# SwiGLU gate and up as seven products of block sums in a transformer block

## Chip, cores and metric

The kernel runs on one core of a Trainium2 chip. The metric is the device time of one execution in microseconds (us). The median of three runs is given; the profile is of one further execution. All arithmetic is in 32-bit floats; matmuls take their operands in the fp32r format.

## The reference

One encoder layer over 512 tokens (plus 16 learned ones that attention alone sees) of width 1024: a norm, a joint projection, two attention branches, gates and an output projection, then the feed-forward part, in which the change lies:

```
hn = rmsnorm(h, norm_ffn_g)                                   # 512 tokens x 1024
h  = h + (silu(hn @ w_ffn_gate) * (hn @ w_ffn_up)) @ w_ffn_down   # D_FF = 2816
y  = rmsnorm(h, norm_final_g)
```

## The kernel before

**Precision by three products.** Every large matmul is made of three: each 32-bit operand is split into a high half (a ScalarE cast to fp32r) and a low half (VectorE: the value less its high half), and `mm3` (L142) adds high x high, high x low and low x high into one PSUM bank. `split` (L73) is the helper that makes the two halves; its cast is L74 and its subtraction L75.

**Weights.** All weights are one list, `stream`, of chunks of 512 KB in the order in which they are used. `stage` (L119) issues a chunk's load on SyncE's queue into one of three buffers `wst`; `weights(key)` (L132) loads STAGE = 5 chunks ahead and splits READY = 2 chunks ahead into one of four pairs of buffers `wh`, `wl`. A chunk of gate (`fg`, f) or up (`fu`, f) holds 1024 rows (8 blocks k of 128) by 128 columns, a chunk of the down projection holds 2 blocks k by 512 columns.

**Stages.** After attention comes the output projection (`accumulate` with "out"): two halves of the output columns, the first in banks of the pool `z`, the second in banks of the pool `mm`. The second half ends token block by token block; each end adds to the residual `hres` (L805), takes the sum of squares (L808) and the reciprocal root (`rstd`), scales to `hn` (L825). `turned(tp)` (L827) transposes half the tokens of `hn` on TensorE, four 128x128 blocks to a bank, and ScalarE (L838) and VectorE (L839) take the bank out as `hT_h` and `hT_l`, 8 blocks k by 512 tokens. Gate and up of feature block 0 (`early`) are computed in two halves of 256 tokens, to fill TensorE's time around the second `turned`.

The feed-forward loop then runs over the other 21 blocks f of 128 features. For each, gate and up are 8 blocks k x 3 matmuls of 512 tokens, 48 in all; ScalarE applies SiLU (L872), VectorE multiplies (L876) and the result is split into `aT_h`, `aT_l`. Last comes the down projection (`accumulate` with "down"): 22 blocks k, 4 token blocks, two halves of the output columns; then the final norm and the stores.

**Order.** Outside a hand-ordered opening, a planner sets the order on each engine: of the instructions that it takes to be ready it issues the one that stands first in the program. `high_priority(offset=EVAC)` moves an instruction ahead. Buffers, and whole pools that take over the space of pools closed before, wait for the release of what they replace. PSUM has four banks under `mm` and two tiles of two banks under `z`.

Of the kernel before, what the change touches and what calls it, by code (L numbers as in the profile page):

```python
# [9 lines left out]
F32 = mybir.dt.float32  # L10
F32R = mybir.dt.float32r
# [5 lines left out]
P = 128  # L17
# [22 lines left out]
def block_kernel(ctx: ExitStack, tc: tile.TileContext, x, meta, norm_mix_g, w_in, w_gate, b_gate,  # L40
# [18 lines left out]
    def tr_tile():  # L59
        return ps_mm.tile([P, 512], F32, tag="mm", name="tr")  # L60
# [52 lines left out]
    for half in range(2):  # L113
        for k0 in range(0, NFF, 2):
            rows(("down", half, k0), w_fd, half * 512, k0)

    staged, loaded = [], {}

    def stage(upto):  # L119
        for n in range(len(staged), min(len(stream), upto)):  # L120
            _, view, c0, cw, k0, k1 = stream[n]
            st = wpool.tile([P, k1 - k0, cw], F32, tag="wst", bufs=3, name="wst")
            staged.append(st)
            for a, b in ((0, 4), (4, 8)) if n < 2 else ((0, k1 - k0),):
                nc.sync.dma_start(st[:, a:b], view[:, k0 + a:k0 + b, c0:c0 + cw])

    def parts(n):
        k, _, _, cw, k0, k1 = stream[n]
        loaded[k] = tuple(wpool.tile([P, k1 - k0, cw], F32R, tag=t, name=t) for t in ("wh", "wl"))
        return loaded[k]  # L130

    def weights(key):  # L132
        at = next(i for i, c in enumerate(stream) if c[0] == key)
        if at < START:
            return loaded[key]
        stage(at + STAGE)
        for n in range(len(loaded), min(len(stream), at + READY)):
            wh, wl = parts(n)
            split(wh, wl, staged[n], nc.gpsimd if n < 3 else None)
        return loaded[key]  # L140

    def mm3(ps, pairs, start=True, stop=True):  # L142
        n = len(pairs)
        for i, (ah, al, bh, bl) in enumerate(pairs):
            nc.tensor.matmul(ps, lhsT=ah, rhs=bh, start=(start and i == 0), stop=False)  # L145
            nc.tensor.matmul(ps, lhsT=ah, rhs=bl, start=False, stop=False)  # L146
            nc.tensor.matmul(ps, lhsT=al, rhs=bh, start=False, stop=(stop and i == n - 1))  # L147

    def proj(ps, w, act, tok, ks=(0, KT)):
        (wh, wl), (ah, al) = w, act  # L150
# [624 lines left out]

    def accumulate(pool, name, act, nk, half, tail, done, banks, pieces=None):

        ah, al = act
# [5 lines left out]
        extra = z_tile()[:, 0] if pieces else None  # L784

        def step(k, t, c0, c1):
            wh, wl = weights((name, half, k // 2 * 2))
            q = slice(t * P, (t + 1) * P)
            mm3((acc[t] if c0 == 0 else extra)[:, c0:c1],
                [(ah[:, k, q], al[:, k, q], wh[:, k % 2, c0:c1], wl[:, k % 2, c0:c1])], k == 0, k == nk - 1)  # L790


        def cuts(t):
# [26 lines left out]
    with tc.tile_pool(name="outp", bufs=1) as op_:  # L820
        hn = op_.tile([P, NQ, D], F32, name="hn")

        def normed(t):
            r = rstd(ssq[t][:, 1:2], more=ssq[t][:, 0:1])()
            nc.vector.tensor_scalar(hn[:, t], hres[:, t], r, None, op0=ALU.mult)  # L825

        def turned(tp):  # L827
            cs = slice(tp * 256, (tp + 1) * 256)
            for k in range(0, KT, 2):
                pt = tr_tile()  # L830
                for i in range(2):
                    for t in range(2):
                        nc.tensor.transpose(pt[:, (2 * i + t) * P:(2 * i + t + 1) * P],  # L833
                                            hn[:, 2 * tp + t, (k + i) * P:(k + i + 1) * P], ident)
                for i in range(2):
                    g = g_ffn[:, k + i:k + i + 1]
                    p = pt[:, i * 256:(i + 1) * 256]
                    nc.scalar.activation(hT_h[:, k + i, cs], p, AF.Copy, scale=g)  # L838
                    nc.vector.scalar_tensor_tensor(hT_l[:, k + i, cs], p, g, hT_h[:, k + i, cs].bitcast(F32),  # L839
                                                   op0=ALU.mult, op1=ALU.subtract)  # L840

        def done(t):
            normed(t)
            if t == 2:
                turned(0)

        accumulate(op_, "out", (mg_h, mg_l), KT, 0, 0, lambda t: None, "z")
        accumulate(op_, "out", (mg_h, mg_l), KT, 1, 6, done, "mm")

        early = [mm_tile(), mm_tile()]  # L850
        for ps, key in zip(early, (("fg", 0), ("fu", 0))):
            proj(ps[:, 0:256], weights(key), hT, slice(0, 256))
        turned(1)
        for ps, key in zip(early, (("fg", 0), ("fu", 0))):
            proj(ps[:, 256:512], weights(key), hT, slice(256, 512))
        use_table("silu_and_others")
    mid.close()


    with tc.tile_pool(name="ffn", bufs=1) as fp:  # L860
        aT_h = fp.tile([P, NFF, SEQ], F32R, name="aT_h")
        aT_l = fp.tile([P, NFF, SEQ], F32R, name="aT_l")
        gF = fp.tile([P, D], F32, name="gF")
        nc.gpsimd.dma_start(gF, norm_final_g.rearrange("(o d) -> o d", o=1).broadcast_to([P, D]))
        for f in range(NFF):
            if f == 0:
                pg, pu = early
            else:
                pg = mm_tile()
                proj(pg, weights(("fg", f)), hT, ALL)  # L870
            sg = fp.tile([P, SEQ], F32, tag="sg", bufs=2, name="sg")
            nc.scalar.activation(sg, pg, AF.Silu)  # L872
            if f:
                pu = mm_tile()
                proj(pu, weights(("fu", f)), hT, ALL)
            nc.vector.tensor_tensor(sg, pu, sg, op=ALU.mult)  # L876
            split(aT_h[:, f], aT_l[:, f], sg)
# [12 lines left out]

        def gained(t, cs):
            if len(outs) == t:
                outs.append(fp.tile([P, D], F32, tag="outs", name="outs", bufs=2))
# [4 lines left out]
        accumulate(fp, "down", (aT_h, aT_l), NFF, 0, 0, lambda t: None, "z")  # L898
        accumulate(fp, "down", (aT_h, aT_l), NFF, 1, 6, finish, "mm", gained)


# [27 lines left out]
```

## Time and profile before

| | us |
|---|---|
| median of 3 runs | 1004.76 (1004.44 to 1005.29) |
| profiled execution, its own time | 1004.22 |
| span of the profile | 1002.5 |
| TensorE busy | 986.8 |
| VectorE busy | 526.5 |
| ScalarE busy | 451.0 |
| first transposes of `hn` to last of gate and up | 625 to 874 |
| down projection to the end | 874 to 1002.5 |

Engines: PE is TensorE, PEld its weight loads, DVE VectorE, ACT ScalarE, POOL GpSimd, SP SyncE; SPq and POOLq are DMA queues. A row of the view by line gives line, engine, operation, written tile <- read tiles, shapes and count, then busy time and the mean of one in ns, then idle time of the engine before them and what ended it. A row of the timeline gives start and duration in us, then the instruction. TensorE's matmuls overlap, so the distance between two starts tells more than one matmul's duration.

### The profile page before, as it was taken

The numbers are of one execution on the slowest core, as the hardware profiler recorded it, in microseconds if no ns is written. First come the engines' busy times: TensorE is split into PE (matmuls) and PEld (weight loads), VectorE is DVE, ScalarE is ACT, GpSimd is POOL, SyncE is SP. The second block draws the span as 40 slices with busy tenths as digits, with TensorE's granted clock in tenths as the row PEclk, the third lists the DMA queues.
The fourth block names the chain that finished last, engine by engine and source line by source line (L and its number), as shares of the span: only waits on it lengthen the run. The fifth ranks groups of instructions, "written<-read, shape, count | busy, mean of one in ns | idle before, by whom it ended". The sixth has DMA issues, their size and how long they took to land.

```text
span 1002.5 us, 14077 instructions
## 1 busy us (share of the span) xinstructions
PE 986.8 (98%) x5529; PEld 855.2 (85%) x5529; DVE 526.5 (53%) x974; ACT 451.0 (45%) x848; POOL 109.9 (11%) x152
## 2 busy tenths in 40 slices
PE   7999999999999999999999999999999999999997
PEld 5999899998889999889878888888888888888886
DVE  7665446667777777777763334633333333312323
ACT  5655564555455666555653333623232232311313
POOL 4000000000122121122013220000000000000103
PEclk9999999999999999999999999999999999999998
DMA  6322222222333332333223352433333333232212
GB/s 198 106 64 63 85 85 63 85 64 64 86 105 86 106 85 65 105 85 86 84 84 85 104 177 76 122 91 103 99 91 105 87 103 103 87 105 88 102 42 85
DMA packets 129733, 93.01 MB, mean 93 GB/s; under 512 B 3681, under 2 KB 114434, under 8 KB 129666
## 3 DMA queue, kind: packets, MB, share of 16 engines
q1 hardware_dynamic: 127506, 85.09, 28.2%
q0 software_dynamic: 2000, 6.95, 2.6%
q8 instruction: 43, 0.70, 0.3%
q14 instruction: 24, 0.20, 0.1%
q10 hardware_dynamic: 160, 0.07, 0.0%
HBM read 85.67 MB, written 2.10 MB: 88 GB/s over the span
## 4 chain that ended last, share of the span: by engine, by line
PE 93%; DVE 3%; ACT 2%; issue 0%; DMA 0%; POOL 0%; SPq 0%; DVEq 0%; ACTq 0%; POOLq 0%
PE mm L145 25%; PE mm L146 24%; PE mm L147 24%; PE z L145 4%; PE z L146 4%; PE z L147 4%; PE tr L301 2%; PE z L432 1%; PE z L433 1%; PE tr L276 1%; PE z L325 0%; PE tr L313 0%; DMA xs<-in_x_dram 0%; PE tr L833 0%; DVE xs L608 0%
## 5 line engine op out<-in xcount | busy, mean ns | idle before, releaser
L75 DVE TENSOR_TENSOR wl<-wst,wh 128x1024 fp32r<-128x1024 f32 x150 | 185.8, 1239 | 256.8 <-ACT wh L74 254.3
L74 ACT CAST wh<-wst 128x1024 fp32r<-128x1024 f32 x150 | 157.9, 1052 | 358.7 <-PE mm L146 267.5
L145 PE MATMUL mm<-xT_h,wh 128*128 128x264 f32 (+2 forms) x776 | 249.1, 321 | 1.0 <-DVE dk L413 0.8
L146 PE MATMUL mm<-xT_l,wh 128*128 128x264 f32 (+2 forms) x776 | 246.9, 318 | 0.4 <-DVE xT_l L619 0.3
L147 PE MATMUL mm<-xT_h,wl 128*128 128x264 f32 (+2 forms) x776 | 246.1, 317 | 0.0
L145 PEld LDWEIGHTS mm<-xT_h,wh 128*128 128x128 f32 x776 | 146.1, 188 | 11.7 <-ACT xT_h L618 1.0
L146 PEld LDWEIGHTS mm<-xT_l,wh 128*128 128x128 f32 x776 | 146.0, 188 | 10.1 <-DVE xT_l L619 0.7
L147 PEld LDWEIGHTS mm<-xT_h,wl 128*128 128x128 f32 x776 | 146.0, 188 | 10.0
L146 PE MATMUL mm<-hT_l,wh 128*128 128x512 f32 (+1 forms) x368 | 139.9, 380 | 0.0
L145 PE MATMUL mm<-hT_h,wh 128*128 128x512 f32 (+1 forms) x368 | 139.7, 380 | 0.1
L147 PE MATMUL mm<-hT_h,wl 128*128 128x512 f32 (+1 forms) x368 | 139.7, 380 | 0.0
L145 PEld LDWEIGHTS mm<-hT_h,wh 128*128 128x128 f32 x368 | 69.0, 188 | 13.6 <-ACT hT_h L838 0.4
L146 PEld LDWEIGHTS mm<-hT_l,wh 128*128 128x128 f32 x368 | 69.2, 188 | 13.2 <-DVE hT_l L839 0.2
L147 PEld LDWEIGHTS mm<-hT_h,wl 128*128 128x128 f32 x368 | 69.2, 188 | 13.1
L145 PE MATMUL mm<-o_h,wh 128*128 128x512 f32 x128 | 53.2, 415 | 0.0
L876 DVE TENSOR_TENSOR sg<-mm,sg 128x512 f32<-128x512 f32 x22 | 15.2, 691 | 70.8 <-PE mm L147 70.8
L146 PE MATMUL mm<-o_l,wh 128*128 128x512 f32 x128 | 50.1, 391 | 0.8 <-DVE o_l L504 0.8
L147 PE MATMUL mm<-o_h,wl 128*128 128x512 f32 x128 | 50.1, 391 | 0.0
L282 POOL COPY v_s<-vT 128x16 f32<-128x16 f32 x64 | 21.8, 369 | 210.0 <-ACT vT L287 210.0
L460 ACT ACTIVATE pr<-pr,nm 128x144 f32<-128x144 f32 (+3 forms) x64 | 36.3, 568 | 14.2 <-DVE nm L458 14.1
L145 PE MATMUL z<-wh,aT_h 128*128 128x512 f32 (+1 forms) x110 | 40.5, 368 | 0.0
L146 PE MATMUL z<-wl,aT_h 128*128 128x512 f32 (+1 forms) x110 | 40.5, 368 | 0.0
(227 smaller groups left out, 1538.3 us busy)
## 6 DMA issues: line engine op xcount, KB each, us to landing
wst<-in_w_in_dram SPq DMA_DIRECT2D x46, 512.0 KB, 3.9
wst<-in_w_ffn_gate_dram SPq DMA_DIRECT2D x22, 512.0 KB, 3.8
wst<-in_w_ffn_up_dram SPq DMA_DIRECT2D x22, 512.0 KB, 3.8
wst<-in_w_ffn_down_dram SPq DMA_DIRECT2D x22, 512.0 KB, 3.6
wst<-in_w_gate_dram SPq DMA_DIRECT2D x16, 512.0 KB, 3.9
dk<-dk POOLq DMA_DIRECT2D x16, 264.0 KB, 4.9
wst<-in_w_br_sb_dram SPq DMA_DIRECT2D x8, 512.0 KB, 3.5
wst<-in_w_br_df_dram SPq DMA_DIRECT2D x8, 512.0 KB, 3.6
```

Of the source, the lines that this page charges most:

```text
L74: (hi_copy or nc.scalar.copy)(hi, src)
L75: (lo_eng or nc.vector).tensor_tensor(lo, src, hi.bitcast(F32), op=ALU.subtract)
L145: nc.tensor.matmul(ps, lhsT=ah, rhs=bh, start=(start and i == 0), stop=False)
L146: nc.tensor.matmul(ps, lhsT=ah, rhs=bl, start=False, stop=False)
L147: nc.tensor.matmul(ps, lhsT=al, rhs=bh, start=False, stop=(stop and i == n - 1))
L276: nc.tensor.transpose(pt[:, j * P:(j + 1) * P], vT[:, j * P:(j + 1) * P], ident)
L282: nc.gpsimd.tensor_copy(v_s[:, 32 * t:32 * t + NM], vT[:, (t + 1) * P:(t + 1) * P + NM])
L301: nc.tensor.transpose(pt[:, (t - j) * P:(t - j + 1) * P], blocks(t, j * P, (j + 1) * P), ident)
L432: nc.tensor.matmul(o, lhsT=q[c][:, qs], rhs=k[c][:, 0, k0:k1], start=True, stop=False)
L433: nc.tensor.matmul(o, lhsT=q[c][:, qs], rhs=k[c][:, 1, k0:k1], start=False, stop=True)
L460: nc.scalar.activation(pr[:, c], pr[:, c], AF.Exp, bias=nm[:, c:c + 1], accum_out=ls[:, t, c:c + 1])
L876: nc.vector.tensor_tensor(sg, pu, sg, op=ALU.mult)
```

## The change

For each feature block f from 1 on, gate and up together are a product of two 2x2 block matrices: rows gate and up by columns K1 and K2 (the first and last four blocks k) on the weights' side, and K1 and K2 by T1 and T2 (the first and last 256 tokens) on the activations' side. Instead of eight block products, seven products of sums are made (the Strassen-Winograd scheme), each of 4 blocks k x 3 matmuls of 256 tokens: 84 matmuls a block f.

- Activations: `turned` also copies each transposed piece, unsplit, to `bf` (16 more ScalarE instructions); `block_sums` makes three sums and one intermediate on VectorE and splits the four operands that are not slices of `hT` or are negated (t2, t1, t3, t4).
- Weights: up is loaded a second time in part: K1 to the tile `s21`, onto which an accumulating DMA from GpSimd's queue adds K2; a second accumulating DMA adds gate's K1 onto up's K1 in its staging tile `wsu`. VectorE makes the other two sums (in `c2` and `c4`). Jobs `c1` to `c4` split gate; s2 and s1; s3 and up's K2; s4.
- Products: `first` (a11·b11, a12·b21), `second` (s2·t2, s1·t1, s3·t3), `third` (a22·t4, s4·b22); the next block's `first` stands between `second` and `third`. One bank, e1, goes through four products in turn and is copied out by ScalarE in between.
- The feed-forward result `aT` is kept unsplit; the down projection splits each block k when it needs it (`act`), in each of its two halves, into 8 buffers `da` of a pool `dw`.

The core of the diff:

```diff
@@ stage
+            if key[0] == "fu" and key[1]:
+                if "w" not in fpools:
+                    return
+                st = fpools["w"].tile([P, KT, P], F32, tag="wsu", bufs=2, name="wsu")
+                s21 = fpools["w"].tile([P, KT, P], F32, tag="s21", bufs=3, name="s21")
+                fpools["s", key[1]] = s21
+            else:
+                st = wpool.tile([P, k1 - k0, cw], F32, tag="wst", bufs=3, name="wst")
...
+            if key[0] == "fu" and key[1]:
+                cs = slice(c0, c0 + cw)
+                nc.sync.dma_start(s21[:, 4:8], view[:, 0:4, cs])
+                nc.gpsimd.dma_start(s21[:, 4:8], view[:, 4:8, cs], accum_op=ALU.add)
+                nc.gpsimd.dma_start(st[:, 0:4], w_fg[:, 0:4, cs], accum_op=ALU.add)
@@ turned, block_sums
+                nc.scalar.activation(bf[k // 4][tp_][:, (k + i) % 4], p, AF.Copy, scale=g)
+    def block_sums():
+        (b11, b12), (b21, b22) = bf
+        sub, add = ALU.subtract, ALU.add
+        nc.vector.tensor_tensor(b11, b11, b12, op=sub)
+        nc.vector.tensor_tensor(b12, b22, b12, op=sub)
+        nc.vector.tensor_tensor(b22, b11, b22, op=add)
+        nc.vector.tensor_tensor(b21, b22, b21, op=sub)
+        th, tl = tsum["t2"]
+        nc.scalar.activation(th, b22, AF.Copy, scale=-1.0)
+        nc.vector.scalar_tensor_tensor(tl, b22, -1.0, th.bitcast(F32), op0=ALU.mult, op1=sub)
+        for n, v in (("t1", b11), ("t3", b12), ("t4", b21)):
+            split(*tsum[n], v)
@@ feed-forward
+        def c1(f):
+            wh, wl = chunk(1)
+            split(wh, wl, staged[at_of["fg", f]])
...
+        def c2(f):
+            g = staged[at_of["fg", f]]
+            s = fpools["s", f]
+            nc.vector.tensor_tensor(s[:, K1], s[:, K2], g[:, K1], op=ALU.add)
+            wh, wl = chunk(2)
+            split(wh, wl, s)
...
+        def c3(f):
+            u = staged[at_of["fu", f]]
+            wh, wl = chunk(3)
+            split(wh, wl, u)
...
+        def c4(f):
+            g, s = staged[at_of["fg", f]], ops[f, "s"]
+            nc.vector.tensor_tensor(g[:, K2], s[:, K1], g[:, K2], op=ALU.add)
+            wh, wl = chunk(4)
+            split(wh[:, K1], wl[:, K1], g[:, K2])
...
+        jobs = [(c1, 1), (c1, 2), (c2, 1), (c3, 1), (c4, 1)]
+        for f in range(2, NFF):
+            jobs += [(c2, f), (c3, f)] + [(c1, f + 1)] * (f + 1 < NFF) + [(c4, f)]
...
+        def first(f):
+            e1, e2, e3 = mm_tile()[:, 0:256], mm_tile()[:, 0:256], z_tile()[:, 0, 0:256]
+            product(f, "a11", "b11", e1, True, True)
+            product(f, "a12", "b21", e2, True, True)
...
+                nc.scalar.copy(q1, e1)
+                nc.vector.tensor_tensor(sg[:, T1], e2, q1, op=ALU.add)
+            nc.scalar.activation(sg[:, T1], sg[:, T1], AF.Silu)
+        def second(f):
+            product(f, "s2", "t2", e1, False, True)
+                nc.scalar.copy(qx, e1)
+            ready(at_job(c3, f) + 2)
+            product(f, "s1", "t1", e3, True, True)
+            product(f, "s3", "t3", e1, False, True)
+                nc.scalar.copy(qy, e1)
+                nc.vector.tensor_tensor(qy, e3, qy, op=ALU.add)
+        def third(f, qx, qy):
+            product(f, "a22", "t4", e1, False, True)
+                nc.vector.scalar_tensor_tensor(aT[:, f, T1], e1, -1.0, sg[:, T1], op0=ALU.mult, op1=ALU.mult)
+            product(f, "s4", "b22", e3, False, True)
+                nc.vector.tensor_tensor(sg[:, T2], e3, qx, op=ALU.add)
+            nc.scalar.activation(sg[:, T2], sg[:, T2], AF.Silu)
+            nc.vector.scalar_tensor_tensor(aT[:, f, T2], qy, -1.0, sg[:, T2], op0=ALU.mult, op1=ALU.mult)
...
+        first(1)
+        ready(4)
+        first(2)
+        for f in range(1, NFF):
+            ready(at_job(c2, f) + 3)
+            rest = second(f)
+            if 1 < f < NFF - 1:
+                ready(at_job(c1, f + 1) + 2)
+                first(f + 1)
+            third(f, *rest)
+            ready(at_job(c4, f) + 2)
@@ down
+        dw = dw_ctx.enter_context(tc.tile_pool(name="dw", bufs=1, reuse_waits="tile"))
+        def act(half, k):
+            m = half * NFF + k
+            for i in range(len(acts), min(2 * NFF, m + 3)):
+                a = dw.tile([P, 2, SEQ], F32R, tag="da", bufs=8, name="da")
+                split(a[:, 0], a[:, 1], aT[:, i % NFF])
+                acts.append(a)
+            return acts[m][:, 0], acts[m][:, 1]
```

Also, `hn` and `bf` lie in the pool `opool` of the stages before, the pool of the output projection's scratch is dropped, and GpSimd's load of the final gain `gF` stands where it stood, ahead of the blocks.

More of the change, by code (lines that the diff above doesn't have):

```diff
@@ L776, in accumulate @@
     def accumulate(pool, name, act, nk, half, tail, done, banks, pieces=None):
-        ah, al = act
         if banks == "z":
@@ L786, in step @@
         def step(k, t, c0, c1):
+            ah, al = act(half, k)
             wh, wl = weights((name, half, k // 2 * 2))
@@ L819, in block_kernel @@
     hT = (hT_h, hT_l)
[L820 to L856, printed above, removed]
@@ new lines, in done, with merged @@
+    def done(t):
+        normed(t)
+        if t == 2:
+            turned(0)
+    def merged(half, k):
+        return mg_h[:, k], mg_l[:, k]
+    accumulate(mgp, "out", merged, KT, 0, 0, lambda t: None, "z")
+    accumulate(mgp, "out", merged, KT, 1, 6, done, "mm")
+    early = [mm_tile(), mm_tile()]
+    for ps, key in zip(early, (("fg", 0), ("fu", 0))):
+        proj(ps[:, 0:256], weights(key), hT, slice(0, 256))
+    turned(1)
+    for ps, key in zip(early, (("fg", 0), ("fu", 0))):
+        proj(ps[:, 256:512], weights(key), hT, slice(256, 512))
@@ L857, in block_kernel @@
+    block_sums()
+    use_table("silu_and_others")
     mid.close()
     with tc.tile_pool(name="ffn", bufs=1) as fp:
-        aT_h = fp.tile([P, NFF, SEQ], F32R, name="aT_h")
-        aT_l = fp.tile([P, NFF, SEQ], F32R, name="aT_l")
+        aT = fp.tile([P, NFF, SEQ], F32, name="aT")
         gF = fp.tile([P, D], F32, name="gF")
         nc.gpsimd.dma_start(gF, norm_final_g.rearrange("(o d) -> o d", o=1).broadcast_to([P, D]))
[L865 to L877, printed above, removed]
```

117 lines of the change are left out of this document (103 added, 14 removed).

## Prediction

> **What bounds the kernel now.** I read the engine totals on the page first, then the chain that ended last, then a table of stretches, then the timeline of the feed-forward stage.
>
> ```profile
> span 1002.5 us, 14077 instructions
> PE 986.8 (98%) x5529; PEld 855.2 (85%) x5529; DVE 526.5 (53%) x974; ACT 451.0 (45%) x848; POOL 109.9 (11%) x152
> ...
> PE 93%; DVE 3%; ACT 2%; issue 0%; DMA 0%; POOL 0%; SPq 0%; DVEq 0%; ACTq 0%; POOLq 0%
> ```
>
> TensorE is busy for 98% of the span and is 93% of the chain. The table of stretches (PE, weight loads, VectorE, ScalarE, GpSimd, then clock, DMA share and GB/s) shows this for the stage that is changed:
>
> ```profile
> core 0: us, PE busy (x) PEld busy (x) DVE busy (x) ACT busy (x) POOL busy (x), PEclk, DMA share, GB/s
> ...
> 625.00:646.00 21.00, 20.75 (x150) 18.85 (x149) 14.94 (x32) 14.72 (x31) 0.60 (x1) 1.00 0.35 101
> ...
> 656.90:874.20 217.30, 217.30 (x961) 179.92 (x960) 74.83 (x80) 63.41 (x81) 0.00 (x0) 1.00 0.33 97
> 874.20:934.00 59.80, 59.80 (x265) 49.55 (x264) 15.89 (x15) 13.84 (x14) 0.35 (x1) 1.00 0.29 97
> ```
>
> From 656.9 to 874.2 us (feature blocks 2 to 21 of gate and up) TensorE has no gap, and VectorE is busy for a third, ScalarE for 29%. The 21 us ahead of it, where the normalized activations are transposed, already have VectorE and ScalarE at 70%. So a cut in TensorE's time is worth its full size in the long stretch, as long as VectorE keeps up, and it must be paid for in the stretch ahead.
>
> **TensorE: the gain.** A block's period now, and the spacing of matmuls of 512 and 256 columns, from the timeline:
>
> ```profile
> 656.86 0.69 DVE L876 TENSOR_TENSOR sg<-mm,sg 128x512 f32<-128x512 f32 x1 [3.42 <-PE mm L147]
> ...
> 874.46 0.69 DVE L876 TENSOR_TENSOR sg<-mm,sg 128x512 f32<-128x512 f32 x1 [3.38 <-PE mm L147]
> ```
> ```profile
> 631.31 0.28 PE L145 MATMUL mm<-hT_h,wh 128*128 128x256 f32 x1
> ...
> 636.94 0.28 PE L147 MATMUL mm<-hT_h,wl 128*128 128x256 f32 x1
> ```
>
> The two products stand 20 blocks apart: 217.60 / 20 = 10.88 us for 48 matmuls of 512 columns, 226.7 ns each. The two matmuls of 256 columns are the first and last of 48 in a row (block 0, gate and up, first half of the tokens): 5.63 / 47 = 119.8 ns, although each load of weights lasts 188 ns; they overlap. After the change a block has 7 products of 4 x 3 matmuls of 256 columns: 84 x 119.8 = 10.06 us. So a half-width matmul costs 53% of a whole one, and one eighth fewer column passes becomes 7.5% less time: 0.82 us a block, for blocks 1 to 21 **-17.2 us**. Block 0 stays as it was.
>
> The Trainium skill (TensorE: Matmul & The Clock Gate, Back-to-back issue gap) gives N/2.4 + 2.5 ns as the gap; by it the blocks would take 10.36 and 9.17 us and the gain would be an estimated 25 us. The rows contradict it at both widths (226.7 and 119.8 against 215.8 and 109.2), so I take the rows.
>
> **VectorE and ScalarE in the steady blocks.** Means by line and shape, from 600 to 800 us:
>
> ```profile
> L75 DVE TENSOR_TENSOR wl<-wst,wh 128x1024 fp32r<-128x1024 f32 x36 | 44.1, 1224 | 62.1 <-ACT wh L74 60.7
> L876 DVE TENSOR_TENSOR sg<-mm,sg 128x512 f32<-128x512 f32 x15 | 10.4, 691 | 47.1 <-PE mm L147 47.1
> L75 DVE TENSOR_TENSOR aT_l<-sg,aT_h 128x512 fp32r<-128x512 f32 x14 | 9.6, 684 | 0.0
> L839 DVE SCALAR_TENSOR_TENSOR hT_l<-tr,pcol,hT_h 128x256 fp32r<-128x256 f32 x16 | 7.5, 482 | 3.0 <-ACT hT_h L838 2.7
> ...
> L74 ACT CAST wh<-wst 128x1024 fp32r<-128x1024 f32 x36 | 38.0, 1055 | 114.0 <-PE mm L146 103.3 <-PE mm L147 6.3 <-PE z L147 4.4
> L74 ACT CAST aT_h<-sg 128x512 fp32r<-128x512 f32 x15 | 9.3, 622 | 0.5 <-DVE sg L876 0.5
> L872 ACT ACTIVATE sg<-mm 128x512 f32<-128x512 f32 x15 | 8.8, 586 | 0.0
> L838 ACT ACTIVATE hT_h<-tr,pcol 128x256 fp32r<-128x256 f32 x16 | 7.3, 478 | 6.9 <-PE tr L833 6.6
> ```
>
> VectorE per block after: three low halves of 1024 (c1, c2, c3) 3.67, one of 512 (c4) 0.68, the two sums left to it 1.38, five evacuations of 256 at 0.48 (L839's row, nearest in shape) 2.4: 8.1 us of 10.06, against 3.8 of 10.88 now. ScalarE: three casts 3.17, one of 512 0.62, three bank copies and two halves of SiLU at 0.48: 6.2 us. Neither is the bound, VectorE by 2 us. The low halves of the activation, 684 ns each, move to the down stage, where each is made twice: 22 more on each engine in 120 us, in stretches where VectorE is busy for a quarter; a block of k lasts 12 x 226.7 = 2.72 us there and needs 0.68 + 0.61. I cost it at nothing but for its first.
>
> The waits inside a block: bank e1 takes four products in turn and is copied out by ScalarE after s2·t2 and s3·t3. The copy (0.28 of the last matmul + 0.48) hides behind s1·t1 (12 x 0.12 = 1.44 us) or the next block's first two products (2.88 us), unless it queues behind a cast of 1.05 us: then 0.28 + 1.05 + 0.48 - 1.56 = 0.25 us shows. A copy can also gain nothing, so 0 to 0.25 a copy; the cover is longer than the copy alone, so I take 0.05 us a block: **+1.0** (0 to 10). In blocks 1 and 21 no next block's products stand between s3·t3 and a22·t4: 2 x 0.85 = **+1.7**.
>
> **The accumulating DMAs.** Each block gets 256 KB more of plain transfer (s21) and two accumulating ones of 256 KB on GpSimd's queue: 1.8 MB in 10.06 us instead of 1 MB in 10.88. At 0.33 share for 97 GB/s, 178 GB/s takes 0.6. No row shows an accumulating DMA; the nearest:
>
> ```profile
> wst<-in_w_ffn_up_dram SPq DMA_DIRECT2D x22, 512.0 KB, 3.8
> ...
> dk<-dk POOLq DMA_DIRECT2D x16, 264.0 KB, 4.9
> ...
> hres<-in_x_dram POOLq DMA_DIRECT2D x4, 512.0 KB, 6.5
> ...
> gF<-in_norm_final_g_dram POOLq DMA_DIRECT2D x1, 512.0 KB, 3.9
> ```
>
> 3.8 to 6.5 us; I take 4.9 (same queue, same size). `wsu` has two buffers, so c3 of block f frees the one that block f+2 loads: plain 3.8, accumulate 4.9, split about 2.5, in two periods of 20.1 us: hidden with 8.9 us to spare. GpSimd's queue holds nothing else in these blocks. **0.**
>
> **The start of the stage: the main cost.** Sixteen copies `bf` join the 16 hT casts on ScalarE, then `block_sums` puts 4 sums and 4 splits of 1024 on VectorE, ahead of the blocks' own weights in program order.
>
> ```profile
> 632.46 0.68 DVE L805 TENSOR_TENSOR hres<-hres,mm 128x512 f32<-128x512 f32 x1
> ...
> 636.08 0.75 DVE L825 TENSOR_SCALAR hn<-hres,rs 128x1024 f32<-128x1024 f32 x1
> ...
> 642.00 0.60 POOL L864 DMA_DIRECT2D gF<-in_norm_final_g_dram  x1 [52.76 <-ACT hT_h L838]
> ...
> 645.69 0.40 PE L145 MATMUL mm<-hT_h,wh 128*128 128x512 f32 x1
> ```
> ```profile
> 634.26 0.20 ACT L226 ACTIVATE rs<-rs 128x1 f32<-128x1 f32 x1
> 637.70 1.94 ACT L838 ACTIVATE hT_h<-tr,pcol 128x256 fp32r<-128x256 f32 x4 [3.24 <-PE tr L833]
> ```
>
> Now block 1 starts at 645.69. If nothing were late, block 1's and 2's first products (2 x 24 x 0.12, both on the untouched hT) would end at 651.45, and s2·t2 would follow. It needs t2 and c2(1), behind this on VectorE: 8 hT_l 3.9, 4 sums 4.9, 4 low halves 4.9, block 0's product 0.7, c1(1) and c1(2) 2.4, an evacuation 0.5, c2(1) 1.9: 19.2 us. It can begin when the last hn is done, 636.83 + about 1.1: the 8 `bf` of the first half of the tokens (8 x 0.48 = 3.8 us) eat ScalarE's idle time before 637.70 (3.24 us) and delay the last rstd. That gives 657.1 with VectorE never idle; I allow 1 us of idling: 658.1, **+6.7**. Lower end +2: the low halves of t1, t3 and t4 (3.7 us) go after c2(1). Upper end +12: gF's issue waited here until 642.00, for the pools whose space it takes over; if it stands ahead of the accumulating DMAs on GpSimd, it waits for the end of the sums (about 655), then 0.6 + 4.9 + 3.2 for accumulation and c2(1): 663.7.
>
> TensorE idles in this, and the clock with it. The table of stretches shows the price near the kernel's start:
>
> ```profile
> 10.00:15.00 5.00, 3.55 (x14) 2.17 (x13) 4.90 (x10) 2.55 (x7) 3.81 (x4) 0.66 0.93 295
> 15.00:20.00 5.00, 4.84 (x35) 4.46 (x36) 4.83 (x15) 4.31 (x12) 2.33 (x2) 1.00 0.38 104
> ```
>
> Clock 0.66 for 5 us is 1.7 us lost: **+1.7** (0 to 3).
>
> **Into the down stage.** Now the matmuls run on without a gap at 874.19. After, act(0)'s split (0.62 + 0.68) waits for its buffer, in the space that the blocks' tiles had. If that space held early tiles, it is done beforehand: 0. If it held `sg`, it follows the last add, SiLU and product: 0.28 + 3 x 0.48 + 1.30 + some 1.3 of handovers between engines and table load = 4.3. I take **+2.0**, near the middle, since no row decides the placement.
>
> **Sum:** -17.2 + 1.0 + 1.7 + 6.7 + 1.7 + 2.0 = -4.1. The profiled execution took 1004.22 us (span 1002.5), 0.54 below the median of the three runs; on the median 1004.76 - 4.1 = **1000.7 us**.
>
> **Rivals.** (1) The start hides: c2(1) is put before the spare low halves, no clock loss, free handover: -17.2 + 2 + 1.7 + 1 = -12.5, 992.3 us. For it: VectorE idles some 2 us of 642 to 646 now. Against: `block_sums` stands first in the program. (2) Slower: e1's copy is queued on ScalarE behind a cast in every block, and VectorE, with 2 us of slack, hands c3 over late; each block then waits. It turns the sign when a block waits 4.1 / 20 = 0.2 us more; at 0.25 for both copies it is +0.5 a block, +9 over the forecast: 1009.7 us. For it: 8.1 of 10.06 us on VectorE, in a fixed order. Against: no deadline shorter than the work before it. (3) The accumulating DMAs pace the blocks: (3.8 + L + 2.5) / 2 exceeds 10.06 once L passes 13.8 us; at L = 17 a block takes 11.65 and the change costs 1004.76 - 4.1 + 20 x 1.6 = 1032 us. Against: 4.9 us on the nearest row. The Trainium skill (SBUF — State Buffer, Who interferes with whom) says that GpSimd-issued DMAs starve while VectorE runs in its 2-port modes; the blocks' VectorE work is of two-input forms, for which it expects no starving, and no run so far shows either.
>
> **How the numbers follow.** About 0.2% (2 us) is what a measurement of this kernel can tell from no change. Forecast 0.50, of which 0.34 faster, 0.12 same, 0.04 slower (its own range, from the ends of the start, 995 to 1007); rival 1 0.22, all faster; rival 2 0.20: 0.07 same, 0.13 slower; rival 3 0.08, slower. Faster 0.56, same 0.19, slower 0.25. The range leaves out rival 3 and the best of rival 1: 991 to 1010.
>
> **What would show it.** Right: matmuls of 256 columns 120 ns apart, 10.1 us from block to block; one hole of 3 to 8 us, in pieces, before s2·t2 of block 1, put down to VectorE's low halves, with the clock below 1 beside it; a gap of up to 4 us before the first down matmul. Wrong: blocks above 10.3 us; waits on `s21` or `wsu` by DMA; a spacing other than 120 ns; act splits that hold the down stage.

## The result and the profile after

The changed kernel is **slower**: 1020.89 us (median of 4 runs, 1019.34 to 1022.40) against 1004.81 before (4 runs beside it), ratio 1.016 with a 95% interval of 1.0142 to 1.0177. The forecast was 1000.7 us, 991 to 1010. The profiled execution took 1022.40 us, its span is 1020.6.

From the page of the changed kernel, the span and the engine totals:

```profile
span 1020.6 us, 16182 instructions
...
PE 979.8 (96%) x6285; PEld 882.8 (86%) x6285; DVE 633.7 (62%) x1172; ACT 543.8 (53%) x1026; POOL 163.8 (16%) x194
```

TensorE is busy 7.0 us less than before while the span is 18.1 us longer, so the loss is idle time, and some of the busy time is matmuls at half speed. The timeline of the changed kernel shows where (rows of PE, DVE, ACT and POOL by time; the bracket is the idle time before the row and what ended it):

```profile
640.53 1.84 POOL L141 DMA_DIRECT2D s<-in_w_ffn_up_dram  x1
...
647.78 0.69 DVE L933 TENSOR_TENSOR s<-s,wst 128x512 f32<-128x512 f32 x1 [5.62 <-DMA s<-in_w_ffn_up_dram]
648.39 1.22 DVE L876 TENSOR_TENSOR bf<-bf 128x1024 f32<-128x1024 f32 x1
649.52 0.87 DVE L869 SCALAR_TENSOR_TENSOR hT_l<-tr,pcol,hT_h 128x256 fp32r<-128x256 f32 x2
...
650.06 0.58 PE L168 MATMUL mm<-hT_l,wh 128*128 128x256 f32 x1 [5.37 <-DVE hT_l L869]
...
661.59 0.28 PE L167 MATMUL mm<-t_h,wh 128*128 128x256 f32 x1
...
680.23 1.05 ACT L74 CAST wh<-wsu 128x1024 fp32r<-128x1024 f32 x1 [4.43 <-DMA wsu<-in_w_ffn_gate_dram]
...
682.28 0.69 DVE L933 TENSOR_TENSOR s<-s,wst 128x512 f32<-128x512 f32 x1 [5.05 <-DMA s<-in_w_ffn_up_dram]
...
687.05 0.58 PE L167 MATMUL mm<-hT_h,wh 128*128 128x256 f32 x1 [4.52 <-ACT qx L998]
...
698.80 0.42 DVE L1016 SCALAR_TENSOR_TENSOR aT<-qy,sg 128x256 f32<-128x256 f32 x1
...
872.59 0.42 DVE L1016 SCALAR_TENSOR_TENSOR aT<-qy,sg 128x256 f32<-128x256 f32 x1
...
878.46 0.28 PE L169 MATMUL z<-hT_h,wl 128*128 128x256 f32 x1
...
882.69 0.79 PE L167 MATMUL z<-wh,da 128*128 128x512 f32 x1 [3.95 <-ACT da L74]
...
1005.84 0.28 PE L169 MATMUL z<-wh,da 128*128 128x256 f32 x1
```

Four things are seen. A **first hole** of 5.4 us: PE's row names the token splits (L869), but in VectorE's order those stand behind an addition of the weight sum (L933), which waited 5.62 us for the accumulating DMA issued at 640.53, and behind one sum of the activations (L876, 1.22 us). A **second hole** of 4.5 us: PE waits for a bank copy (`qx`), and both ScalarE and VectorE had just waited for accumulating DMAs. A **gap** of 4 us before the first down matmul. And a **tail**: 14.8 us from the last matmul to the end of the span, where before had 7.5, by its row

```profile
994.95 0.28 PE L147 MATMUL z<-wh,aT_l 128*128 128x256 f32 x1
```

The table of stretches of the changed kernel (columns as in the prediction: PEclk, then DMA share and GB/s last; a share above 1 means that the recorded times of the packets add up to more than the engines' time) shows what follows each hole:

```profile
645.00:650.00 5.00, 0.00 (x0) 0.00 (x0) 2.22 (x4) 0.36 (x1) 1.28 (x1) 0.86 1.42 178
650.00:655.00 5.00, 4.64 (x18) 4.07 (x19) 4.68 (x7) 3.54 (x8) 0.00 (x0) 0.50 0.06 8
...
685.00:690.00 5.00, 2.95 (x14) 2.95 (x15) 4.04 (x6) 1.83 (x4) 0.00 (x0) 0.61 1.09 243
690.00:695.00 5.00, 5.00 (x33) 5.00 (x33) 1.54 (x3) 1.57 (x3) 2.55 (x2) 0.70 0.69 128
...
750.00:800.00 50.00, 49.18 (x411) 48.78 (x410) 34.20 (x54) 26.72 (x45) 12.80 (x10) 1.00 0.92 184
...
880.00:885.00 5.00, 2.31 (x6) 1.79 (x7) 3.79 (x6) 4.44 (x8) 0.00 (x0) 0.57 0.66 209
```

Behind each of the three holes (the two in the blocks and the gap) matmuls start at about half the rate for some 5 to 6 us, with a granted clock of 0.50 to 0.70 in these stretches: TensorE is "busy" from 650 to 655 with 18 matmuls recorded, where full stretches have some 42 to 45. The steady blocks are not whole either: 49.18 us of 50, and the DMA engines 0.92 busy at 184 GB/s, where the prediction had estimated 0.6. ScalarE by line in the last 36 us of the changed kernel, and what VectorE waited for there:

```profile
L246 ACT ACT_TABLE_LOAD x4 | 5.1, 1283 | 0.1
L248 ACT ACT_TABLE_LOAD x4 | 5.1, 1283 | 0.1
```
```profile
DVE rs L257 <- ACT rs L248: 11.6, 4, 2.9
```

Each of the four token blocks loads one table for the Ln and another for the Exp of its norm. In the planned order the load of the common table by hand (L66) had slipped ahead of the last block's last SiLU (at 871.75 us), which then loaded its own table again (at 879.76).

Against the forecast's own marks (its span would have been 1002.5 - 4.1 = 998.4):

| stretch (us) | forecast | after | difference that arose in it |
|---|---|---|---|
| to s2·t2 of block 1 (658.1 + 1.7 of clock) | 659.8 | 661.6 | +1.8 |
| from there to the end of gate and up (forecast 874.2 - 6.1) | 868.1 | 878.6 | +8.7 |
| handover: length until the first down matmul | 2.0 | 4.1 | +2.1 |
| length from the first to the last down matmul | 120.8 | 123.2 | +2.4 |
| length of the tail | 7.5 | 14.8 | +7.2 |
| sum | | | +22.2 (the spans: +22.2) |

### The profile page after: what moved, and what is told of

It is laid out like the page before. It is cut to its first block, busy times and chain, and to the rows that moved or that the text cites. A ratio compares the mean times of both kernels' runs of the same rounds, so it can differ in the third digit from the quotient of the medians.

```text
span 1020.6 us, 16182 instructions
## 1 busy us (share of the span) xinstructions
PE 979.8 (96%) x6285; PEld 882.8 (86%) x6285; DVE 633.7 (62%) x1172; ACT 543.8 (53%) x1026; POOL 163.8 (16%) x194
## 5 line engine op out<-in xcount | busy, mean ns | idle before, releaser
L75 DVE TENSOR_TENSOR wl<-wst,wh 128x1024 fp32r<-128x1024 f32 (+1 forms) x150 | 174.4, 1163 | 150.1 <-ACT wh L74 149.7
L74 ACT CAST wh<-wst 128x1024 fp32r<-128x1024 f32 (+1 forms) x150 | 147.7, 990 | 168.1 <-PE mm L168 112.2
L167 PE MATMUL mm<-hT_h,wh 128*128 128x256 f32 x284 | 83.1, 295 | 6.9 <-ACT qx L998 6.5
L168 PE MATMUL mm<-hT_l,wh 128*128 128x256 f32 x284 | 83.0, 293 | 5.7 <-DVE hT_l L869 5.7
L169 PE MATMUL mm<-hT_h,wl 128*128 128x256 f32 x284 | 82.3, 290 | 0.2 <-DVE wl L75 0.2
L167 PEld LDWEIGHTS mm<-hT_h,wh 128*128 128x128 f32 x284 | 55.8, 197 | 9.3 <-ACT qx L998 8.0
L142 POOL DMA_DIRECT2D wsu<-in_w_ffn_gate_dram x21 | 26.9, 1283 | 144.9 <-DMA wsu<-in_w_ffn_up_dram 78.4
L167 PE MATMUL mm<-t_h,wh 128*128 128x256 f32 x168 | 47.4, 282 | 0.5 <-ACT qy L1003 0.5
L168 PE MATMUL mm<-t_l,wh 128*128 128x256 f32 x168 | 47.2, 281 | 0.0
L169 PE MATMUL mm<-t_h,wl 128*128 128x256 f32 x168 | 47.0, 281 | 0.0
```

Of the source, the lines that this page charges most:

```text
L74: (hi_copy or nc.scalar.copy)(hi, src)
L75: (lo_eng or nc.vector).tensor_tensor(lo, src, hi.bitcast(F32), op=ALU.subtract)
L142: nc.gpsimd.dma_start(st[:, 0:4], w_fg[:, 0:4, cs], accum_op=ALU.add)
```

## The experiments

Each ran beside the kernel before (1004.46 to 1004.76 us); ratios are to it, and differences in the text are to the changed kernel's 1020.89. Traces are of one execution each; the changed kernel's was the slowest of its four (1022.40), so differences between spans come out up to 1.5 us larger than those between medians.

**1. The table load behind the last SiLU.** The last weight splits are placed ahead of `third` of block 21 in the program; the planner then sets the load by hand last.

```diff
+            if f == NFF - 1:
+                ready(at_job(c4, f) + 2)
             third(f, *rest)
```


> Only the place of the exp/log table load changes: it is planned behind the last block's last SiLU instead of ahead of it. Theory (the changed kernel's tail is long because ScalarE then loads a table for each Ln and each Exp, two loads of 1.28 us per block of 128 tokens): the loads at the Ln and Exp lines vanish, the time from the last matmul to the end falls from 14.8 us to about 7.7, one load less lies in the handover to the down projection (up to -0.5), total -7.1 to -7.6, 1013.3 us. Rival (the tail is long for another cause, such as the output's transfers or VectorE's part of the norm): the loads vanish but the tail stays above 12 us and the total moves by less than 2 us.

1016.26 us (1015.55 to 1016.62), ratio 1.0115 [1.0098, 1.0132]. ScalarE by line in the tail has no load left, only the functions themselves, and the last matmul starts at 1007.28 in a span of 1014.8: a tail of 7.5 us. The load by hand now stands at 881.87, behind the last SiLU (881.43).

```profile
L246 ACT ACTIVATE rs<-ssq 128x1 f32<-128x1 f32 x4 | 1.2, 294 | 0.1
...
L248 ACT ACTIVATE rs<-rs 128x1 f32<-128x1 f32 x4 | 0.8, 203 | 0.1
```

The cause is shown: -7.3 us in the tail. The total gained less than expected (4.6): in the traces the spans differ by 5.8, as this execution took 1.4 us longer up to the last matmul, and the rest is the changed kernel's slow profiled execution. The Trainium skill (ScalarE: Activation LUTs, What ACT_TABLE_LOAD costs) gives about 1283 ns for a load of any set; the rows of the changed kernel agree to the nanosecond. It adds a drain of 1380 ns, which the changed kernel's tail does not show: the next load followed 1.6 us after the first, with an instruction of 0.29 us between.

**2. Early splits for the down projection.** Three `da` tiles take the buffers of weight sums no longer needed and are split before `third` of block 21; later ones rotate through those and three more.

```diff
+        def da(i):
+            tag = ("s21", "s21", "wsu", "s21", "wsu", "da", "da", "da")[i % 8]
+            pool = dw if tag == "da" else fw
...
+            if f == NFF - 1:
+                for i in range(3):
+                    da(i)
             third(f, *rest)
```


> The first splits of the activations for the down projection get buffers of their own (those of the weight sums that the last block no longer needs), so they need not wait for the last block's last VectorE instruction. Theory (the 4.2 us before the first down matmul and the half-speed matmuls right behind it, 0.426 us apart for some 5 us, both come from that wait): the gap falls below 1 us and the down stage's first matmuls are 0.213 to 0.24 us apart, -4.2 for the gap and -1.5 to -2.5 for the clock, total 1014.5 to 1015.5 us. Rival A (the low clock there comes with the change from 256 to 512 columns, not from the gap): the gap goes but the slow matmuls stay, 1016.7. Rival B (the weights of the down projection are late as well): the gap stays at 3 us or more, 1019 to 1021.

1016.71 us (1016.53 to 1016.94), ratio 1.0122 [1.0107, 1.0137]. No gap is left, and the same stretch is at full clock with 23 matmuls of 512 instead of 6:

```profile
880.00:885.00 5.00, 5.00 (x23) 3.98 (x22) 4.28 (x8) 4.53 (x7) 0.00 (x0) 1.00 0.49 170
```

So the low clock came from the gap (rival A falls), and the weights were not late (rival B falls). The total gained 4.2, a little less than expected; spans differ by 5.9.

**3 and 4. Sums of the first blocks on VectorE.** The two accumulating DMAs are left out for blocks 1 and 2, then for 1 to 5.

```diff
+                if key[1] <= 2:        # then: <= 5
+                    continue
...
+            if f <= 2:                 # then: <= 5
+                u = staged[at_of["fu", f]]
+                nc.vector.tensor_tensor(s[:, K2], u[:, K1], u[:, K2], op=ALU.add)
+                nc.vector.tensor_tensor(u[:, K1], u[:, K1], g[:, K1], op=ALU.add)
             nc.vector.tensor_tensor(s[:, K1], s[:, K2], g[:, K1], op=ALU.add)
```


> Blocks 1 and 2 alone form the two weight sums with VectorE additions (two more of 0.69 us a block) and have no accumulating transfer. Theory (the first hole, 5.65 us, and the half-speed matmuls behind it, stand because an addition that waits for the accumulating transfer lies ahead of the last token splits in VectorE's fixed order): the hole falls below 1.5 us, s2*t2 of block 1 starts by 657.5 instead of 661.6, -4 to -8 us; the second hole (4.8 us, for the sums of blocks 3 to 5) stays or moves; total 1013 to 1017. Rival (VectorE's backlog of token sums is the cause, as the forecast had it): two more additions make it worse or leave it, hole 5 us or more, 1020 to 1023.

> As the run before, for blocks 1 to 5. Theory (both holes are waits for accumulating transfers at the head of VectorE's and ScalarE's orders, and the clock falls to half behind each): both holes below 1.5 us together 2.5, no half-speed stretch in blocks 1 to 3, -12 to -16 us, 1005 to 1009. Rival A (backlog of VectorE): no gain beyond 2 us, since VectorE gets 7 us more work in five blocks. Rival B (the single loads are late as well, because two buffers and the fixed orders let them start late): the first hole goes, the second stays at 3 us or more, 1010 to 1014.

1017.12 us (ratio [1.0107, 1.0137]) and 1014.44 us ([1.0086, 1.0116]). With two blocks the first hole is gone, s2·t2 of block 1 starts at 656.1 instead of 661.6, and the second hole stays at 4.4 us; with five, both are gone, as TensorE's longest waits in the feed-forward stage's first 60 us show:

```profile
641.18 0.39 PE L170 MATMUL mm<-hT_l,wh 128*128 128x256 f32 x1 [1.08 <-DVE hT_l L871]
...
677.52 0.39 PE L171 MATMUL mm<-t_h,wl 128*128 128x256 f32 x1 [1.63 <-DVE wl L75]
```

VectorE got more work and TensorE waited less, so VectorE's backlog was not the first hole's cause (the forecast's reading). But the totals gained 3.8 and 6.4 us where 4 to 8 and 12 to 16 were expected. One reason lies in the trace with five blocks: the granted clock is 0.50 there too, for 3.4 us, some 1.7 us lost, although no hole before it is longer than 1.1 us:

```profile
643.00:646.40 3.40, 3.40 (x18) 3.40 (x17) 2.67 (x5) 1.14 (x4) 0.00 (x0) 0.50 0.02 5
```

The next two runs give another.

**5 and 6. Plain transfers in place of accumulating ones; and all sums on VectorE.**

```diff
-                nc.gpsimd.dma_start(s21[:, 4:8], view[:, 4:8, cs], accum_op=ALU.add)
-                nc.gpsimd.dma_start(st[:, 0:4], w_fg[:, 0:4, cs], accum_op=ALU.add)
+                nc.gpsimd.dma_start(s21[:, 4:8], view[:, 4:8, cs])
+                nc.gpsimd.dma_start(st[:, 0:4], w_fg[:, 0:4, cs])
```


> The two transfers from GpSimd's queue stay, with the same waits and sizes, but overwrite instead of adding (so the weight sums hold only one summand). Theory (it is the second transfer in series, issued from GpSimd only when the first has landed, that is late, not the adding): first hole 4.5 to 6 us, second 3.5 to 5, total 1019 to 1021.5. Rival (adding makes the transfer slow): landing falls from 4.7 and 5.8 us to the 3.5 to 4 of plain ones, the holes shrink by 1.5 us or more each, total below 1017.

The other run has the diff of 3 and 4 for every block:

> All 21 blocks form both weight sums on VectorE (two more additions of 0.69 us a block, VectorE from about 34 to 41 us in 50) and no accumulating transfer is left. Theory (the accumulating transfers cost only where they come late, in the first blocks; later blocks are paced by TensorE and by the copy of the second product's bank on ScalarE): from the third to the twentieth block 174 to 176 us as with the sums of five blocks moved (174.7), total 1013 to 1016. Rival A (they load the transfer queues and slow every block): those 17 blocks fall below 172.5, total 1012 or less. Rival B (VectorE becomes too full): above 177, total above 1017.

1013.57 us ([1.0071, 1.0098]) and 1010.59 us ([1.0040, 1.0066]). Both theories fell, and the first rival and rival A hold: the adding itself is dear. But it is not all: with plain transfers the two holes shrink from 5.4 and 4.5 us to

```profile
648.47 0.39 PE L168 MATMUL mm<-hT_l,wh 128*128 128x256 f32 x1 [3.69 <-DVE hT_l L869]
...
684.16 0.39 PE L167 MATMUL mm<-hT_h,wh 128*128 128x256 f32 x1 [2.19 <-ACT qx L998]
```

so most of the first and half of the second remain. VectorE still waits there at L933, 3.9 and 4.0 us, for `s21`; without the second transfers (runs 4 and 6) both holes are gone, so in the first blocks it also costs that these come late. DMA issues from 700 to 850 us, first of the changed kernel, then of the one with plain transfers (count, KB each, median us to landing):

```profile
wst<-in_w_ffn_gate_dram SPq DMA_DIRECT2D x14, 512.0 KB, 5.2
wsu<-in_w_ffn_gate_dram POOLq DMA_DIRECT2D x15, 256.0 KB, 4.6
s<-in_w_ffn_up_dram POOLq DMA_DIRECT2D x14, 256.0 KB, 5.8
```
```profile
wst<-in_w_ffn_gate_dram SPq DMA_DIRECT2D x14, 512.0 KB, 4.2
wsu<-in_w_ffn_gate_dram POOLq DMA_DIRECT2D x15, 256.0 KB, 3.6
s<-in_w_ffn_up_dram POOLq DMA_DIRECT2D x14, 256.0 KB, 3.7
```

The stretch from 750 to 800 us, with plain transfers and then with all sums on VectorE:

```profile
750.00:800.00 50.00, 50.00 (x421) 50.00 (x420) 35.91 (x55) 27.56 (x46) 7.50 (x10) 1.00 0.67 185
```
```profile
750.00:800.00 50.00, 50.00 (x421) 50.00 (x420) 41.84 (x65) 27.60 (x45) 0.00 (x0) 1.00 0.36 105
```

Much the same traffic, 185 and 184 GB/s, keeps the DMA engines 0.67 busy when it overwrites and 0.92 when it adds, and the plain loads of the gate weights beside it land in 5.2 instead of 4.2 us. The size of the packets is not the reason: from 700 to 850 us the accumulating transfers go in packets of 497 B and take 5.4% of the engines' time per MB, SyncE's plain loads go in packets of 503 B and take 2.5%, and the plain transfers from GpSimd's queue, in packets of 3.3 KB, 2.3%. VectorE's addition at L933 waits for the loads of the gate weights in nearly every block. The waits from 700 to 860 us, changed kernel, then plain transfers:

```profile
DVE s L933 <- DMA wst<-in_w_ffn_gate_dram: 35.8, 15, 3.3
...
PE mm L167 <- ACT qx L998: 1.8, 4, 0.8
```
```profile
DVE s L933 <- DMA wst<-in_w_ffn_gate_dram: 14.6, 14, 2.3
```

With 2.4 us a block, the SiLU and the casts behind the addition come late and now and then so does the copy `qx`; with 1.0 us TensorE waits for nothing. From the third block to the twentieth the changed kernel takes 872.59 - 698.80 = 173.8 us, and with all sums on VectorE

```profile
687.41 0.42 DVE L1022 SCALAR_TENSOR_TENSOR aT<-qy,sg 128x256 f32<-128x256 f32 x1
...
858.32 0.42 DVE L1022 SCALAR_TENSOR_TENSOR aT<-qy,sg 128x256 f32<-128x256 f32 x1
```

170.9 us, 10.05 a block: the forecast's 84 x 119.8 ns. With plain transfers it is 170.2 us, so in these blocks the second transfers cost nothing and the adding costs some 3.6 us. Runs 3 and 4 kept the accumulating DMAs in all or most of these blocks (174.9 and 174.7 us).

**7. All sums on GpSimd.** The diff of 3 and 4 for every block, with `nc.gpsimd` for the two new additions.

> All 21 blocks form both weight sums on GpSimd (two additions of about 1.3 us a block, by the profile's rows for its 128x512 additions) and no accumulating transfer is left. Theory as in the run before: no first and second hole, VectorE not loaded, 17 blocks in 173.5 to 175.5 us, total 1012 to 1015. Rival (VectorE waits for GpSimd's sum at the head of its order as it waited for the transfer): the first hole stays at 2 to 3 us, with half-speed matmuls behind it, total 1015 to 1018.

1012.40 us ([1.0066, 1.0093]), the total that the theory had, but by other parts: the 17 blocks took 170.6 us, less than its 173.5 to 175.5, and as the rival had it a first hole of 2.0 us stays (at 642.20), with matmuls 0.21 us apart from 642.6 to 647.5. The trace has something else, VectorE's low halves from 700 to 860 us:

```profile
L75 DVE TENSOR_TENSOR wl<-s,wh 128x1024 fp32r<-128x1024 f32 x16 | 35.9, 2246 | 1.0 <-ACT wh L74 1.0
L75 DVE TENSOR_TENSOR wl<-wsu,wh 128x1024 fp32r<-128x1024 f32 x16 | 19.5, 1220 | 1.4 <-ACT wh L74 0.9
```

The same instruction on the same shape takes 2246 ns where GpSimd's second addition runs beside it, and 1220 elsewhere. That addition on GpSimd takes 1.80 us, the first one, alone, 1.29.

**8. What waits at the head of VectorE's order.** In blocks 1 to 3 the additions that use `s21` (L933, L947) go to GpSimd; the accumulating DMAs stay. L947 has the same edit as L933.

```diff
-            nc.vector.tensor_tensor(s[:, K1], s[:, K2], g[:, K1], op=ALU.add)
+            (nc.gpsimd if f <= 3 else nc.vector).tensor_tensor(s[:, K1], s[:, K2], g[:, K1], op=ALU.add)
```


> The accumulating transfers stay as they are; in blocks 1 to 3 the two additions that use the sum they make are done on GpSimd instead of VectorE, so that nothing that waits for a transfer stands ahead of the token splits in VectorE's order. Theory (a late transfer costs time only by its place at the head of an order): hole 1 falls from 5.65 us below 1.5, -4 to -7 us; hole 2 (a ScalarE cast and a later addition) stays at 3 to 5 us, total 1014 to 1017. Rival (the token splits are late for VectorE's own load, or block 1 then stalls for its sum anyway): holes of 4 us or more in sum before s2*t2 of block 1, total 1018.5 or more.

1020.07 us ([1.0139, 1.0170]), no clear gain, as the rival had it. The hole ahead of the token splits is gone, but a new one stands 10 us later:

```profile
651.32 3.75 DVE L75 TENSOR_TENSOR wl<-s,wh 128x1024 fp32r<-128x1024 f32 x1 [2.26 <-ACT wh L74]
...
652.22 1.75 POOL L933 TENSOR_TENSOR s<-s,wst 128x512 f32<-128x512 f32 x1
...
654.99 2.28 DVE L878 TENSOR_TENSOR bf<-bf 128x1024 f32<-128x1024 f32 x1
...
659.87 0.58 PE L167 MATMUL mm<-hT_h,wh 128*128 128x256 f32 x1 [4.94 <-DVE sg L990]
```

VectorE's subtraction takes 3.75 and the sum 2.28 us while GpSimd adds. The move cured one wait and made another, so this run does not tell queue order from lateness by itself. Unexpectedly the second hole shrank to 1.0 us too: VectorE's wait at L933 is 3.4 instead of 5.05 us there. The blocks from 3 to 20 took 2.0 us more than in the changed kernel, which was not taken apart. The Trainium skill (SBUF — State Buffer, Who interferes with whom) says that a VectorE instruction with two inputs in SBUF contends with a GpSimd instruction that reads SBUF; both of these runs agree (1.22 against 2.25 to 3.75 us). The prediction used the part of that section on DMA issue; this is the part that bears.

**9. Three buffers for the up weights.**

```diff
-                st = fpools["w"].tile([P, KT, P], F32, tag="wsu", bufs=2, name="wsu")
+                st = fpools["w"].tile([P, KT, P], F32, tag="wsu", bufs=3, name="wsu")
```


> The accumulating transfers stay as they are; only the staging of the up weights gets three buffers instead of two, so that the third block's up weights need not wait for the first block's to be split. Theory (the second hole stands because the third block's two transfers in series can start only behind that split, and ScalarE's cast for it heads its order): hole 1 stays at 5 to 6.5 us, hole 2 falls from 4.8 to below 1.5 us with its half-speed matmuls, total 1014 to 1016.5. Rival (the transfers of the gate and up sums are late on their own, VectorE's 5.05 us wait for the fifth block's sum above all): hole 2 stays at 3 us or more, total 1019 to 1022.

1024.42 us ([1.0184, 1.0212]), 3.5 worse. ScalarE's cast no longer waits for a DMA, and the second hole is as long as ever:

```profile
678.68 1.05 ACT L74 CAST wh<-wsu 128x1024 fp32r<-128x1024 f32 x1 [0.99 <-PE mm L168]
...
684.33 0.69 DVE L933 TENSOR_TENSOR s<-s,wst 128x512 f32<-128x512 f32 x1 [5.16 <-DMA s<-in_w_ffn_up_dram]
...
689.10 0.58 PE L167 MATMUL mm<-hT_h,wh 128*128 128x256 f32 x1 [4.68 <-ACT qx L998]
```

The rival holds: what decides the second hole is VectorE's wait at its addition for the sum of block 5, by its place in the planned order three blocks ahead. The first hole grew to 6.7 us: with one more set of transfers at the start the accumulating ones land in 7.9 and 8.4 us there instead of 6.0 and 7.1.

**10. The three edits together** (1, 2, and sums of blocks 1 to 5 on VectorE).

> The three edits together: load of the exp/log table behind the last SiLU, early splits for the down projection, sums of blocks 1 to 5 on VectorE. Theory (the three losses are separate and add): spans fell by 5.8, 5.9 and 7.8 us alone, so 19.5 us together, span 1001 and time 1001 to 1003, faster than before (1004.5) by 0.1 to 0.4%. Rival (they overlap, what one gives back is lost at the next): 1004 to 1008.

1001.40 us (999.75 to 1001.66), ratio 0.9964 [0.9951, 0.9976]: faster than before, within the theory's 1001 to 1003. The total fell by 19.5 us, as the three spans had fallen together (5.8 + 5.9 + 7.8); the three medians had fallen by 15.3 together, so the losses are separate, and at least add.

**11 and 12. A better version.** Edits 1 and 2, all sums on VectorE but the second of blocks 1 and 2 on GpSimd, three buffers for `wsu` and two for `s21` (the early splits' tiles follow suit), and no loading of the SiLU table by hand.

```diff
-                st = fpools["w"].tile([P, KT, P], F32, tag="wsu", bufs=2, name="wsu")
-                s21 = fpools["w"].tile([P, KT, P], F32, tag="s21", bufs=3, name="s21")
+                st = fpools["w"].tile([P, KT, P], F32, tag="wsu", bufs=3, name="wsu")
+                s21 = fpools["w"].tile([P, KT, P], F32, tag="s21", bufs=2, name="s21")
...
+            nc.vector.tensor_tensor(s[:, K2], u[:, K1], u[:, K2], op=ALU.add)
+            (nc.gpsimd if f <= 2 else nc.vector).tensor_tensor(u[:, K1], u[:, K1], g[:, K1], op=ALU.add)
...
-    use_table("silu_and_others")
```


> All sums on VectorE (in blocks 1 and 2 the second one on GpSimd), three buffers for the up weights and two for the sums, the exp/log load behind the last SiLU, early splits for the down projection, and no load of the SiLU table by hand. Theory (the losses are separate): 1010.6 with all sums on VectorE, less the 13.0 us by which the two other edits lowered the kernel with five blocks' sums on VectorE (1014.4 to 1001.4), less 2.6 us of the second block (12.7 us instead of 10.03), less up to 1.3: 994 to 997.5. Rival (they overlap): 998 to 1001.

The last run has the second sum on GpSimd in all blocks; "the kernel before" in its text is run 11.

> As the kernel before, but with the second sum on GpSimd in all 21 blocks. Theory (TensorE paces the blocks at 10.03 us and VectorE has room): within 1 us of the kernel before. Rival A (VectorE still sets waits): 1 to 3 us less. Rival B (additions on GpSimd slow VectorE's own): 1 to 4 us more.

Run 11: **995.69 us** (995.63 to 995.93), within its theory's 994 to 997.5; ratio 0.9911 [0.9897, 0.9924]: 0.9% faster than before, 2.5% faster than the changed kernel. Run 12: 997.12 (ratio 0.9928 [0.9915, 0.9940]), 1.4 us more, as rival B had it; its low halves of `wsu`, which GpSimd's addition overlaps in part, take 1353 ns against 1224. The page and the timeline of run 11:

```profile
span 993.9 us, 16029 instructions
...
PE 973.5 (98%) x6285; PEld 878.7 (88%) x6285; DVE 660.8 (66%) x1212; ACT 532.7 (54%) x1016; POOL 113.0 (11%) x154
```
```profile
863.96 0.28 PE L171 MATMUL z<-hT_h,wl 128*128 128x256 f32 x1
864.08 0.40 PE L169 MATMUL z<-wh,da 128*128 128x512 f32 x1
```

Gate and up end 10 us earlier than before (874.2) and the down projection follows 0.12 us later; its first three matmuls already ran at 860.5. The seven products do save TensorE time; the change lost it, and more, elsewhere.

## Why the prediction was wrong, step by step

Of the 22.2 us by which the span missed the forecast, 10.5 arose up to the end of gate and up, 4.5 in the handover and the slow matmuls behind it, and 7.2 in the tail. Two steps failed above all: the accumulating DMAs and the tail were both put at nothing.

- **TensorE's gain, -17.2:** right. 10.05 us a block by the run with all sums on VectorE, 10.06 forecast; 120 ns between matmuls.
- **Steady waits, +1.0:** after took 10.22 us a block between blocks 3 and 20, some 2 us more than 17 x (10.06 + 0.05) in all. Inside the range given (0 to 10), but the cause was not a copy queued behind a cast alone: VectorE's addition waited for loads that the accumulating DMAs had slowed; with plain transfers the same blocks took 170.2 us. In blocks 1 and 21, costed at +1.7, TensorE's waits for the copy `qy` are 0.2 and 0.5 us.
- **Accumulating DMAs, 0: this step failed.** Landing was sized nearly right for the steady blocks (4.9 taken; 4.6 and 5.8 measured) and too low for the start (6.3 and 6.4 from 640 to 700 us), and the budget of two periods for `wsu` does hold there. Missing were three things: only `wsu` was costed, not `s21`, whose sum VectorE needs first and which takes two transfers in series (6.0 and 7.1 us for the first three); cover was counted in block periods, while the planned order puts the additions up to three blocks ahead, at the head of VectorE's order, so that a wait holds the splits of other work; and the DMA share was scaled by bytes (0.6 instead of 0.92). In the first blocks, where the staging of several blocks starts at once, this made both holes: without the second transfers (experiments 4 and 6) both are gone.
- **Start, +6.7 and clock, +1.7:** the sum is only 1.8 short, and that is luck. VectorE's low halves were named; experiment 3 gave VectorE more and the hole went. With all sums on VectorE s2·t2 starts at 655.3, at full clock: 3.8 us behind 651.45, the mark for nothing being late, where the forecast counted 8.4. Clock below 1 behind the hole was right.
- **The second hole** was in no term: 4.5 us and about 2.7 of half speed (47 matmuls recorded from 687 to 695 us, where 70 would run).
- **Handover, +2.0:** the bad end (4.3) came, 4.1 measured, as all first splits waited for the last VectorE instruction. The clock behind it, 2.4, was costed only at the start.
- **Tail, 0:** not costed at all. The planned order put a table load ahead of the last SiLU, 7.2 us. The prediction counted the moved SiLU work but not where `use_table` would land in the new order.
- **Rivals:** rival 3 named the right part but the wrong mechanism (blocks paced by a transfer of over 13.8 us). "Waits on `s21` or `wsu` by DMA" and "act splits that hold the down stage" were listed as signs that the prediction is wrong, and both stand in the trace.

What stays open: experiments 3 and 4 gained less than the holes and half-speed stretches they removed. With five blocks moved, block 3 ends 8.8 us earlier, where the two holes and the slow matmuls behind them had cost some 15. A half-clock stretch at 643 us (1.7) and steady blocks 0.9 us longer than the changed kernel's explain some of it; the rest was not taken apart.

## What to carry to other kernels

A transfer that "has time" has it only if nothing with a near deadline stands behind its first reader in that engine's fixed order: look up the order, not the distance in blocks. Cost every hole of 4 us on TensorE with the half-speed matmuls behind it (some 2.5 us each here). When instructions are added or moved, look where hand-placed table loads end up relative to the functions of the other set.

## What the runs showed of the hardware

- Adding in the DMA costs: the same traffic (184 and 185 GB/s) keeps the DMA engines 0.92 busy against 0.67, transfers of 256 KB land in 4.6 and 5.8 against 3.6 and 3.7 us, each MB takes 5.4% of the engines' 150 us against 2.3 to 2.5%, and plain loads beside them slow from 4.2 to 5.2 us.
- VectorE's additions and subtractions of two f32 tiles in SBUF (128x1024) take 2.2 to 3.8 us instead of 1.22 where GpSimd's additions run beside them (runs 7 and 8), and GpSimd's (128x512) 1.80 instead of 1.29 (run 7).
- TensorE's clock fell to half behind every hole of 3.6 to 6.7 us in these runs, and not behind those of 1.0 to 2.2 us in blocks 2 to 4. The Trainium skill (TensorE: Matmul & The Clock Gate, What's actually happening) has the clock fall after an idle window of about 3.4 us; the long holes agree with it. But a hole that long is not needed here: between the second transposes, with no hole over 1.2 us (2.0 in run 7), the clock also fell to 0.50 for 3.4 us in runs 4, 10 and 11 and for some 7 in run 7, and did not in run 6 with holes of the same size.
